# A two-layer hybrid diffusion block on one core: the order of TensorE's work in the attention stage

## The chip, the cores and the metric

The kernel runs on one core of a Trainium2 chip. The metric is the device time of one execution in microseconds; the time before is the median of three runs. The engines are named as in the profile: PE (TensorE matmul), DVE (VectorE), ACT (ScalarE), POOL (GpSimd), and SP, whose queue issues the DMAs.

## The reference

Two layers over 1024 latent and 256 context tokens of width 1024. Each layer: a modulated RMSNorm, one input projection whose columns are split among three groups, and one output projection with a gated residual.

```python
(xq, xk, xv, xz_a, xb, xa, xq_a, xkv_a, xz_b, xh, xbg, xcg, xz_c) = split_in(hx @ w_in)
...
o_ax, _, _ = gdn_bidir(*gdn_prepare(xq, xk, xv, xb, xa, ...), s_f, s_b)
a_x = gdn_output(o_ax, xz_a, gdn_norm_g)
...
k_x, v_x = mla_keys_values(xkv_a, mla_kv_norm_g, mla_w_kvb, cos, sin)
q_x = mla_queries(xq_a, mla_q_norm_g, mla_w_qb, cos, sin)
b_x = softmax_attention(q_x, concat([k_x, k_c]), concat([v_x, v_c])) * jax.nn.silu(xz_b)
c_x = conv_branch(xh, xbg, xcg, xz_c, conv_w)
x = x + gate_x * (concat([a_x, b_x, c_x]) @ w_out)
```

Group A is a gated delta recurrence (4 heads of 128, run forward and backward over chunks, the state handed from chunk to chunk). Group B is latent attention: 4 heads, 64 + 32 key columns, 64 value columns; latent queries read 1280 keys, and in the first layer the 256 context queries read the 256 context keys. Group C is a gated convolution. The second layer leaves the context rows out after the keys.

## The kernel before, in words

One Python program writes the instructions through the Tile framework, whose scheduler then orders each engine's instructions by its own estimate of when each is ready. The order in which the program writes them comes from the class `Sched` (L86): the main course of the program calls `sch.tick(us)` with its estimate of PE time, and every side lane (a Python generator: the recurrence, query rows, output weights, attention's ends) that is due runs on to its next `yield us`.

The attention stage goes by units: a query group of `GROUPS` (latent queries 0 to 511, 512 to 1023, context queries) times a pair of heads. Layer 0 has six units, layer 1 four. Per unit:

- `q_head` makes the query operand `qt` (hi and lo parts, 96 rows). Row 96 holds the shift: minus the largest score of the query.
- `a_max` (L1065 on) is the maxima pass: for each tile of 128 queries and each head, one matmul per key group (L1072) and a DVE reduction each (L1074), then a reduction over the groups (L1075) into `nm`. The maxima of the next unit are made during this one, two or three tiles after a step.
- `a_shift`: per head, four (context: two) PE transposes of one 128x1 column (L1082), and one ACT copy of 1x512 into row 96 of `qt` (L79 by its helper). It stands after the unit's last step.
- `a_scores` goes over the keys in steps of two key tiles: for two tiles and two heads, three matmuls (L84 by the helper `mm3`) and an exponential on ACT (L1096) into `probT`. A unit has five steps; a context unit has one.
- `a_pv`, called for a step after the scores of the next one: four V products (L1109), in which the two heads of a pair write to different column halves (`tile_position`), and the row sums: `probT` is added into `vt[5]` for head 0 on DVE (L1122) and into `vt[6]` for head 1 on POOL (L1120), 74 instructions each.
- `a_out` ends a unit as a lane: two ones products sum `vt` over its partitions (L1132), DVE takes the reciprocal (L1135) and multiplies (L1136), POOL multiplies by the gate (L1137), SP stores (L1138).

Beside this run two lanes of the recurrence (`recur`, one for each direction), with their PE groups at L1184, L1194, L1204, L1209 and L1210 and DVE work at L1186, L1196 and L1213. Each chunk has three handovers, with a `yield` after each:

```python
                    for h in range(4):
                        T.matmul(p3[:, h], lhsT=kq("k", h, i), rhs=Sd[:, h], start=True, stop=True)
                    for h in range(4):
                        V.scalar_tensor_tensor(out=X[:, h], in0=p3[:, h], scalar=negeg[:, i, g0 + h:g0 + h + 1], in1=X[:, h],
                                               op0=ALU.mult, op1=ALU.add)
...
                    yield 2.8
```

In the last units of a stage the recurrence has ended, and `load_wo` and `ahead` split the output projection's weights into hi and lo parts (ACT L75, POOL L76 as `wo_lo`) and start the projection.

Of the kernel before, what the change touches and what calls it, by code (L numbers as in the profile page):

```python
# [7 lines left out]
F32 = mybir.dt.float32  # L8
# [20 lines left out]
def kernel(  # L29
# [286 lines left out]
    for l in range(DEPTH):  # L316
# [539 lines left out]
        def q_head(g, h):  # L856
# [19 lines left out]
            Q[g, h] = dict(qt=qt, nm=st([128, 4], "st", name="nm"))  # L876
# [188 lines left out]
        def a_max(g, h, j):  # L1065
            q = Q[g, h]
            mx = st([128, 4], "st", name="mx")
            for gk, (t0, n) in enumerate(GROUPS):
                if g == 2 and gk < 2:
                    continue  # L1070
                pb = bank()
                T.matmul(pb[:, 0:n], lhsT=q["qt"][0:96, 0, j * 128:(j + 1) * 128],  # L1072
                         rhs=kh[0:96, h, t0:t0 + n] if gk < 2 else kc[0:96, 0, h, :], start=True, stop=True)
                V.tensor_reduce(mx[:, gk:gk + 1], pb[:, 0:n], AX.X, ALU.max)  # L1074
            V.tensor_reduce(q["nm"][:, j:j + 1], mx[:, 2 if g == 2 else 0:3], AX.X, ALU.max, negate=True)  # L1075

        def a_shift(g, h):
            q = Q[g, h]
# [6 lines left out]
        def a_scores(u, kts):  # L1085
# [12 lines left out]
            return pts  # L1098

        def a_pv(u, kts, pts):  # L1100
# [22 lines left out]

        def a_out(u):
# [4 lines left out]
            yield 1.5  # L1129
# [8 lines left out]
            S.dma_start(out=bx_d[pair, :, t0:t0 + n], in_=zb)  # L1138

# [12 lines left out]
        def recur(d):  # L1152
# [17 lines left out]
            for s, i in enumerate(order[d]):  # L1170
# [10 lines left out]
                if s:  # L1181
# [9 lines left out]
                    yield 2.8  # L1191
# [9 lines left out]
                yield 2.6  # L1201
# [28 lines left out]


        sch.add(recur(0), recur(1))
        units = [dict(g=g, pair=p) for g in qgs for p in range(2)]

# [3 lines left out]
        def maxes(u):  # L1238
            for j in range(GROUPS[u["g"]][1] // 128):
                for g, h in heads(u):  # L1240
                    yield a_max(g, h, j)

        def warm(u, vs):
# [3 lines left out]
            mg = maxes(u)  # L1247
            for i in vs:
                next(mg, None)
                v_tile(i)  # L1250
                sch.tick(0.9)
            for _ in mg:
                sch.tick(0.6)
# [14 lines left out]
        for u in units[:1 if last else 2]:  # L1268
            for gh in heads(u):
                a_shift(*gh)  # L1270
# [99 lines left out]
        prev = None  # L1370
        for x_, u in enumerate(units):
            g = u["g"]
            keys = a_keys(g)
            steps = [keys[q:q + 2] for q in range(0, len(keys), 2)]
            warmed = 1 if last else 2
            nxt = units[x_ + 1] if warmed <= x_ + 1 < nu else None
            mg = maxes(nxt) if nxt else None
            for q, kts in enumerate(steps):
                pts = a_scores(u, kts)
# [8 lines left out]
                if nxt:  # L1388
                    if q == 0:
                        sch.until(lambda: nxt["g"] in QA)  # L1390
                        for gh in heads(nxt):
                            q_head(*gh)
                        sch.tick(2.4)
                        if nxt["pair"] == 1 and nxt["g"] == 0:
                            sch.add(q_rows(1))
                    many = 8 if len(steps) == 1 else (0, 2, 3, 3, 0)[q]
                    for _ in range(many):
                        next(mg)
                        sch.tick(0.6)
                    if q == len(steps) - 1:  # L1400
                        for gh in heads(nxt):
                            a_shift(*gh)
# [4 lines left out]
        sch.add(a_out(prev[0]))  # L1407
        Q.clear()
        ahead(2)
        sch.tick(1.8)  # L1410
# [91 lines left out]
```

## Time and profile before

| | before |
|---|---|
| median of 3 runs | 1791.59 us (1791.51 to 1793.09) |
| the profiled execution, its own time | 1793.27 us |
| span of the profiled execution | 1791.6 us |
| mean granted TensorE clock | 0.979 of full speed |
| PE busy | 1720.9 us, 96% of the span |
| DVE busy | 1159.8 us, 65% |
| ACT busy | 766.1 us, 43% |
| POOL busy | 609.5 us, 34% |

The span is what the profile shows between the first and the last instruction; the execution's own time has 1.7 us more around it. Busy shares are averages over all stages. The attention stage of layer 0 lies at about 553 to 850 us, that of layer 1 at about 1419 to 1691 us. In rows of the trace a matmul with fp32 operands can appear as two records, and "x2" counts records; a group's busy time counts an overlap once.

### The profile page before, as it was taken

Reading aid. Unit: us, or ns where it says so; the run is one execution under the profiler, and the core shown is the slowest. Engines: PE = TensorE matmul, PEld = TensorE weight load, DVE = VectorE, ACT = ScalarE, POOL = GpSimd, SP = SyncE. Lnnn points to the kernel's source line nnn. Section 1 sums busy time; section 2 is a strip of 40 time slices with the busy share of each in tenths; the row PEclk is TensorE's granted clock in tenths of the full one; section 3 lists DMA queues with packets and bytes.
Section 4 is the critical chain, followed back from the end, with each engine's and each line's share of the span. In section 5 each row is a group of like instructions: output and inputs, shape, how many; then the busy total and the mean of one; then the engine's idle time right before and its main releaser. Section 6 shows DMA issues by size and latency. Waiting matters only on the chain.

```text
span 1791.6 us, 30054 instructions
## 1 busy us (share of the span) xinstructions
PE 1720.9 (96%) x11058; PEld 1336.6 (75%) x11058; DVE 1159.8 (65%) x2144; ACT 766.1 (43%) x1895; POOL 609.5 (34%) x811
## 2 busy tenths in 40 slices
PE   7999999999998799999999999998999889999998
PEld 5887887778888577664788987777787676776586
DVE  2445668887635766875666346689885487768565
ACT  4634663223436243254355435651244543424432
POOL 1510435222212232566431212463113323526741
PEclk9999999999999899999999999999999889999999
DMA  9333556552336446522543313556434524455541
GB/s 353 122 113 99 176 168 191 194 189 88 110 126 215 157 129 186 169 95 88 194 136 107 105 54 130 181 177 208 149 103 123 190 92 144 155 175 160 156 155 59
DMA packets 194578, 265.09 MB, mean 148 GB/s; under 512 B 50304, under 2 KB 114432, under 8 KB 194432
## 3 DMA queue, kind: packets, MB, share of 16 engines
q1 hardware_dynamic: 194432, 263.18, 45.3%
q8 instruction: 87, 1.43, 0.3%
q14 instruction: 59, 0.48, 0.1%
HBM read 183.76 MB, written 79.36 MB: 147 GB/s over the span
## 4 chain that ended last, share of the span: by engine, by line
PE 53%; DVE 5%; ACT 2%; issue 2%; DMA 2%; POOL 1%; SPq 0%; POOLq 0%; DVEq 0%; ACTq 0%
PE bank L84 20%; PE bank L448 13%; PE bank L1109 6%; PE bank L1072 2%; PE bank L1204 2%; PE bank L1194 2%; PE bank L1210 2%; PE bank L1209 2%; PE bank L1184 1%; DVE mx L1074 1%; DVE pr L676 1%; DVE Mb L677 1%; PE bank L512 1%; PE bank L1132 1%; DMA mb_d<-dg 1%
## 5 line engine op out<-in xcount | busy, mean ns | idle before, releaser
L448 PE MATMUL bank<-h_hi,w 128*128 128x512 f32 x1664 | 431.9, 402 | 2.5 <-DVE h_hi L283 2.5
L448 PEld LDWEIGHTS bank<-h_hi,w 128*128 128x128 f32 x1664 | 304.6, 189 | 74.8 <-issue 4.5
L448 PE MATMUL bank<-h_lo,w 128*128 128x512 f32 x832 | 217.7, 402 | 0.0
L448 PEld LDWEIGHTS bank<-h_lo,w 128*128 128x128 f32 x832 | 154.5, 190 | 37.2 <-issue 1.6
L462 DVE SCALAR_TENSOR_TENSOR acc<-pad,col,acc 128x1284 f32<-128x1284 f32 (+1 forms) x104 | 160.1, 1539 | 8.5 <-ACT acc L459 6.8
L1096 ACT ACTIVATE probT<-bank 128x512 f32<-128x512 f32 (+1 forms) x168 | 96.4, 590 | 129.0 <-PE bank L84 123.8
L84 PE MATMUL bank<-wo_hi,mix 128*128 128x512 f32 x576 | 142.8, 398 | 0.0
L84 PEld LDWEIGHTS bank<-wo_hi,mix 128*128 128x128 f32 x576 | 106.8, 188 | 25.5 <-issue 0.8
L1109 PE MATMUL bank<-probT,vt 128*64 128x512 f32 (+1 forms) x336 | 121.4, 601 | 1.1 <-ACT probT L1096 1.1
L76 DVE TENSOR_TENSOR w<-wr,w 128x1024 fp32r<-128x1024 f32 x52 | 66.4, 1279 | 85.2 <-ACT w L75 85.1
L1074 DVE TENSOR_REDUCE mx<-bank 128x1 f32<-128x512 f32 (+1 forms) x200 | 106.8, 588 | 12.8 <-PE bank L1072 11.9
L448 PE MATMUL bank<-h_c,w 128*128 128x256 f32 x816 | 109.5, 287 | 0.0
L1120 POOL TENSOR_TENSOR vt<-vt,probT 128x512 f32<-128x512 f32 x64 | 91.0, 1422 | 48.3 <-ACT probT L1096 45.7
L448 PEld LDWEIGHTS bank<-h_c,w 128*128 128x128 f32 x816 | 102.4, 190 | 6.2 <-issue 4.1
L1190 POOL TENSOR_TENSOR ring<-ring,qx 128x512 f32<-128x512 f32 x32 | 40.9, 1278 | 156.0 <-DMA ring<-row_d 121.9
L84 PE MATMUL bank<-qt,kh 97*128 97x512 f32 (+1 forms) x256 | 86.3, 419 | 3.3 <-ACT qt L79 3.2
L75 ACT ACTIVATE w<-wr 128x1024 fp32r<-128x1024 f32 x52 | 54.9, 1060 | 74.4 <-PE bank L448 55.4
L1122 DVE TENSOR_TENSOR vt<-vt,probT 128x512 f32<-128x512 f32 x64 | 68.3, 1068 | 18.7 <-ACT probT L1096 17.6
L1213 DVE SCALAR_TENSOR_TENSOR ring<-ring,gtot,bank 128x128 f32<-128x128 f32 x144 | 47.3, 345 | 42.6 <-PE bank L1209 33.6
L84 PE MATMUL bank<-wo_lo,mix 128*128 128x512 f32 x288 | 73.9, 395 | 0.0
L677 DVE TENSOR_TENSOR Mb<-Mb,pr 128x31 f32<-128x31 f32 (+15 forms) x186 | 68.8, 370 | 5.0
L676 DVE TENSOR_TENSOR pr<-L,Mb 128x31 f32<-128x31 f32 (+15 forms) x186 | 68.5, 368 | 4.5
(305 smaller groups left out, 3328.4 us busy)
## 6 DMA issues: line engine op xcount, KB each, us to landing
wr<-in_w_blk_dram SPq DMA_DIRECT2D x52, 512.0 KB, 4.0
wa<-in_w_ada_dram SPq DMA_DIRECT2D x32, 512.0 KB, 5.1
gcb<-row_d SPq DMA_DIRECT2D x20, 512.0 KB, 5.1
nn_d<-N SPq DMA_DIRECT2D x20, 512.0 KB, 3.3
ring<-vr_d SPq DMA_DIRECT2D x40, 256.0 KB, 2.6
ring<-nn_d SPq DMA_DIRECT2D x40, 256.0 KB, 3.4
ring<-kt_d SPq DMA_DIRECT2D x40, 256.0 KB, 5.1
qk_d<-gcb SPq DMA_DIRECT2D x18, 512.0 KB, 3.5
```

The source lines that it names most:

```text
L75: A.activation(out=hi, in_=raw, func=ACTF.Copy)
L76: eng.tensor_tensor(out=lo, in0=raw, in1=hi.bitcast(F32), op=ALU.subtract)
L84: T.matmul(outp, lhsT=lh, rhs=rh, start=q == 0, stop=q == n - 1)
L448: T.matmul(pb[:, 0:n], lhsT=self.w[:, wi, k, :], rhs=hg[g][hi][:, k, :], start=q + k == 0, stop=q == 2 and k == KD - 1)
L462: V.scalar_tensor_tensor(out=acc[:, 2:hi], in0=pad[:, 2 + t - r:hi + t - r], scalar=col[:, ci:ci + 1], in1=acc[:, 2:hi], op0=ALU.mult, op1 ...
L676: V.tensor_tensor(out=pv, in0=bc(L[:, 0:k, k], w), in1=N[:, k:k + 1, k:32].to_broadcast([128, k, w]), op=ALU.mult)
L677: V.tensor_tensor(out=N[:, 0:k, k:32], in0=N[:, 0:k, k:32], in1=pv, op=ALU.subtract)
L1074: V.tensor_reduce(mx[:, gk:gk + 1], pb[:, 0:n], AX.X, ALU.max)
L1096: A.activation(out=pts[r][:, kk, 0:n], in_=pb, func=ACTF.Exp)
L1109: T.matmul(u["po"][64 * r:64 * r + 64, 0:n], lhsT=vx[:, kt, hh * 64:hh * 64 + 64], rhs=pts[r][:, kk, 0:n], start=kt == keys[0], stop=kt == ...
L1120: P.tensor_tensor(acc, a0, a1, ALU.add)
L1122: V.tensor_tensor(out=acc, in0=a0, in1=a1, op=ALU.add)
```

## The change

In six parts:

1. PE's order is the order of the program from the moment when the recurrence lanes start until the attention stage has ended (`tc.manual_schedule` on PE). The other engines are ordered by the scheduler as before.
2. The maxima pass becomes a generator that stops after each key group's matmul. `filler` issues two of its matmuls after every score product of steps 1 to 3 (six in a context unit). The ticks are per score product.
3. `a_shift` is one transpose for both heads of a unit (a tile `nm` of 128 x 8), one ACT copy into `rw`, and two DMAs on SP's queue that write row 96 of `qt`. It stands ahead of the scores of the last step.
4. The row sums of both heads go to POOL (130 instructions), but those of head 0 in a unit's last step (18 on DVE).
5. `a_out` is no lane: its first part is called after the unit's last V products, its second (the sums matmul and what follows) ahead of the next V products.
6. The recurrence's yields are 3.4 and 3.0 in place of 2.8 and 2.6.

```diff
-        def a_shift(g, h):
-            q = Q[g, h]
-            n = GROUPS[g][1]
+        def a_shift(u):
+            m = GROUPS[u["g"]][1] // 128
             pn = bank()
-            for j in range(n // 128):
-                T.transpose(pn[0:1, j * 128:(j + 1) * 128], q["nm"][:, j:j + 1], ident)
-            copy_a(q["qt"][96:97, 0, 0:n], pn[0:1, 0:n])
+            T.transpose(pn[0:2 * m, 0:128], u["nm"][:, 0:2 * m], ident)
+            rw = st([8, 128], "h5", F32R, name="rw")
+            copy_a(rw[0:2 * m], pn[0:2 * m, 0:128])
+            for r, gh in enumerate(heads(u)):
+                S.dma_start(out=Q[gh]["qt"][96:97, 0, 0:128 * m].bitcast(F32).rearrange("p (j t) -> p j t", j=m), in_=rw[r * m:(r + 1) * m].bitcast(F32))
...
                     A.activation(out=pts[r][:, kk, 0:n], in_=pb, func=ACTF.Exp)
-                sch.tick(0.0028 * n)
+                    sch.tick(0.0014 * n)
+                    filler()
...
-                    if r:
+                    if kts[-1] == keys[-1] and r == 0:
+                        V.tensor_tensor(out=acc, in0=a0, in1=a1, op=ALU.add)
+                    else:
                         P.tensor_tensor(acc, a0, a1, ALU.add)
-                    else:
-                        V.tensor_tensor(out=acc, in0=a0, in1=a1, op=ALU.add)
...
-                    yield 2.8
+                    yield 3.4
...
-                yield 2.6
+                yield 3.0
...
         sch.add(recur(0), recur(1))
+        in_order = tc.manual_schedule(engines={mybir.EngineType.PE})
+        in_order.__enter__()
...
+            def filler():
+                if nxt and (len(steps) == 1 or 1 <= q <= 3):
+                    for _ in range(6 if len(steps) == 1 else 2):
+                        if next(mg, u) is not u:
+                            sch.tick(0.25)
...
+                if nxt and q == 4:
+                    a_shift(nxt)
+                pts = a_scores(u, kts, filler)
                 if prev:
+                    if ending:
+                        next(ending)
+                        ending = None
                     a_pv(*prev)
                     if prev[0] is not u:
-                        sch.add(a_out(prev[0]))
+                        ending = a_out(prev[0])
+                        next(ending)
...
+        in_order.__exit__(None, None, None)
```

Three pieces of the order show what that moves. In the rows a count stands at the end where an instruction repeats.

The first is PE in layer 0, at the end of the unit of latent queries 512 to 1023 and head pair 0: its last scores (L84), the shift (L1082, after L1088), the maxima (L1072, after L1077) and the V products (L1109, after L1119). Before:

```order
L84 MATMUL bank<-qt,kc 128x512 x12
L1082 MATMUL bank<-cst,nm 1x128 x3
L1109 MATMUL bank<-probT,vt 64x512
L1082 MATMUL bank<-cst,nm 1x128 x3
L1109 MATMUL bank<-probT,vt 64x512
L1082 MATMUL bank<-cst,nm 1x128
L1109 MATMUL bank<-probT,vt 64x512
L1082 MATMUL bank<-cst,nm 1x128
L1109 MATMUL bank<-probT,vt 64x512
```

and with the change:

```order
L84 MATMUL bank<-qt,kl 128x512
L1077 MATMUL bank<-kh,qt 128x512
L1077 MATMUL bank<-kc,qt 128x256
L1119 MATMUL bank<-probT,vt 64x512 x4
L1088 MATMUL bank<-cst,nm 8x128
L84 MATMUL bank<-qt,kc 128x512 x12
L1119 MATMUL bank<-probT,vt 64x512 x4
L84 MATMUL bank<-qt,kh 128x512 x2
L84 MATMUL bank<-qt,kl 128x512
```

The four V products of a step stand together, and one transpose ahead of the last scores takes the place of eight behind them. Over both stages the V products of before stand in 96 runs (64 single products, 15 of two, 5 of three, 9 of four, 1 of seven, 2 of eight); with the change in 40 (38 of four, 2 of eight).

The second is POOL in the last unit of layer 0: the row sums (L1120, after L1132), the gate (L1137, after L1147, first for the unit before, then for this one), and the output weights' splits (L76). Before:

```order
L1120 TENSOR_TENSOR vt<-probT 128x512
L1120 TENSOR_TENSOR vt<-vt,probT 128x512 x3
L1137 TENSOR_TENSOR zb<-zb,vt 128x512
L1120 TENSOR_TENSOR vt<-vt,probT 128x512 x4
L76 TENSOR_TENSOR mix<-raw,mix 128x512
L1120 TENSOR_TENSOR vt<-vt,probT 128x512
L76 TENSOR_TENSOR wo_lo<-wr,wo_hi 128x512 x5
L1137 TENSOR_TENSOR zb<-zb,vt 128x512
```

and with the change:

```order
L1132 TENSOR_TENSOR vt<-probT 128x512
L1132 TENSOR_TENSOR vt<-vt,probT 128x512 x2
L1132 TENSOR_TENSOR vt<-probT 128x512
L1132 TENSOR_TENSOR vt<-vt,probT 128x512 x2
L1147 TENSOR_TENSOR zb<-zb,vt 128x512
L1132 TENSOR_TENSOR vt<-vt,probT 128x512 x11
L76 TENSOR_TENSOR mix<-raw,mix 128x512
L76 TENSOR_TENSOR wo_lo<-wr,wo_hi 128x512 x3
L1147 TENSOR_TENSOR zb<-zb,vt 128x512
L76 TENSOR_TENSOR wo_lo<-wr,wo_hi 128x512 x3
```

Seventeen adds stand where nine stood, and five splits of weights move behind more of them.

The third is PE in layer 0 in the unit of latent queries 0 to 511 and head pair 0, where a recurrence group (L1184, after L1195) hands over through DVE to the next (L1194, after L1205). Before:

```order
L1184 MATMUL bank<-ring_5654,kx 128x128 x5
L1109 MATMUL bank<-probT,vt 64x512
L1184 MATMUL bank<-ring_5654,kx 128x128
L1109 MATMUL bank<-probT,vt 64x512
L1184 MATMUL bank<-ring_5654,kx 128x128 x2
L1072 MATMUL bank<-kh,qt 128x512
L1109 MATMUL bank<-probT,vt 64x512
L1072 MATMUL bank<-kh,qt 128x512
L1109 MATMUL bank<-probT,vt 64x512
L1072 MATMUL bank<-kc,qt 128x256
L1072 MATMUL bank<-kh,qt 128x512 x2
L1072 MATMUL bank<-kc,qt 128x256
```

and with the change:

```order
L1195 MATMUL bank<-ring_5654,kx 128x128 x8
L1077 MATMUL bank<-kh,qt 128x512
L84 MATMUL bank<-qt,kh 128x512 x2
L84 MATMUL bank<-qt,kl 128x512
L1077 MATMUL bank<-kc,qt 128x256
L1077 MATMUL bank<-kh,qt 128x512
L84 MATMUL bank<-qt,kh 128x512 x2
L84 MATMUL bank<-qt,kl 128x512
L1077 MATMUL bank<-kh,qt 128x512
L1077 MATMUL bank<-kc,qt 128x256
L1119 MATMUL bank<-probT,vt 64x512 x4
L1205 MATMUL bank<-ring_5653,ring_5654 128x128 x4
```

The recurrence group is no longer mixed with V products, and what stands between it and the next is fixed.

## Rows read from the trace of the kernel before

**Rows 1.** Page, busy time and share of each engine over the span.
```profile
PE 1720.9 (96%) x11058; PEld 1336.6 (75%) x11058; DVE 1159.8 (65%) x2144; ACT 766.1 (43%) x1895; POOL 609.5 (34%) x811
```

**Rows 2.** Windows: length, busy PE PEld DVE ACT POOL, clock, DMA share, GB/s.
```profile
553.00:632.00 79.00, 60.94 (x393) 51.03 (x392) 55.42 (x132) 29.80 (x79) 17.04 (x15) 0.87 0.58 198
...
781.00:824.00 43.00, 43.00 (x151) 21.53 (x149) 34.80 (x56) 25.69 (x64) 38.18 (x31) 1.00 0.39 123
824.00:850.00 26.00, 26.00 (x88) 10.38 (x88) 14.55 (x15) 9.03 (x16) 14.14 (x11) 1.00 0.22 71
1419.00:1466.00 47.00, 34.20 (x172) 27.70 (x173) 38.12 (x78) 24.61 (x57) 15.42 (x12) 0.79 0.49 158
```

**Rows 3.** Both stages' V products by form; windows of the last units.
```profile
L1109 PE MATMUL bank<-probT,vt 128*64 128x512 f32 x160 | 60.9, 612 | 1.1 <-ACT probT L1096 1.1
...
L1109 PE MATMUL bank<-probT,vt 128*64 128x512 f32 x160 | 57.7, 611 | 0.0
...
781.00:824.00 43.00, 17.59 (x40) 3.53 (x40) 1.00 0.39 123
824.00:850.00 26.00, 14.33 (x40) 3.10 (x40) 1.00 0.22 71
```

**Rows 4.** Timeline of PE in a step with scattered V products: start, us, instruction.
```profile
804.08 1.07 PE L1109 MATMUL bank<-probT,vt 128*64 128x512 f32 x2
805.08 0.49 PE L1072 MATMUL bank<-kh,qt 96*128 96x512 f32 x1
...
806.62 0.73 PE L1072 MATMUL bank<-kh,qt 96*128 96x512 f32 x2
807.29 1.07 PE L1109 MATMUL bank<-probT,vt 128*64 128x512 f32 x2
...
810.29 2.96 PE L84 MATMUL bank<-qt,kc 97*128 97x512 f32 x12
813.09 0.49 PE L1082 MATMUL bank<-cst,nm 128*1 128x128 f32 x3
```

**Rows 5.** Timeline of PE where four V products stand in a row.
```profile
1480.15 1.94 PE L1109 MATMUL bank<-probT,vt 128*64 128x512 f32 x8
1482.02 0.33 PE L846 MATMUL bank<-cst,mq 128*128 128x128 f32 x1
```

**Rows 6.** Groups by form, the shift's transposes in layers 0 and 1.
```profile
L1082 PE MATMUL bank<-cst,nm 128*1 128x128 f32 x40 | 7.4, 298 | 3.7 <-DVE nm L1075 3.7
...
L1082 PE MATMUL bank<-cst,nm 128*1 128x128 f32 x32 | 4.6, 272 | 0.0
```

**Rows 7.** The shift's ACT copies by form, and PE's timeline in layer 1's opening.
```profile
L79 ACT ACTIVATE qt<-bank 1x512 fp32r<-1x512 f32 x6 | 3.5, 584 | 4.3 <-PE bank L1082 4.2
...
1464.13 1.12 PE L84 MATMUL bank<-qt,kh 97*128 97x512 f32 x2 [2.05 <-ACT qt L79]
```

**Rows 8.** DVE and POOL groups by form, 640 to 850; POOL's adds.
```profile
L1122 DVE TENSOR_TENSOR vt<-vt,probT 128x512 f32<-128x512 f32 x32 | 34.4, 1076 | 9.0 <-ACT probT L1096 8.5
L1074 DVE TENSOR_REDUCE mx<-bank 128x1 f32<-128x512 f32 x48 | 31.3, 682 | 3.1 <-PE bank L1072 2.8
L1213 DVE SCALAR_TENSOR_TENSOR ring<-ring,gtot,bank 128x128 f32<-128x128 f32 x56 | 18.5, 346 | 18.2 <-PE bank L1209 15.4
...
L1074 DVE TENSOR_REDUCE mx<-bank 128x1 f32<-128x256 f32 x24 | 10.0, 416 | 1.8 <-PE bank L1072 1.8
...
L1120 POOL TENSOR_TENSOR vt<-vt,probT 128x512 f32<-128x512 f32 x31 | 43.7, 1409 | 18.5 <-ACT probT L1096 17.1
L76 POOL TENSOR_TENSOR wo_lo<-wr,wo_hi 128x512 fp32r<-128x512 f32 x11 | 15.6, 1427 | 5.7 <-ACT wo_hi L75 5.5
...
L1120 POOL TENSOR_TENSOR vt<-vt,probT x64: 1261/1283/1778, 655.4 to 1685.3; 128x512 f32<-128x512 f32 x64
```

**Rows 9.** DMA issues (KB, us to landing); SP's waits, 760 to 870.
```profile
bx_d<-zb SPq DMA_DIRECT2D x8, 256.0 KB, 2.0
...
SPq L1138 <- POOL zb L1137: 22.2, 2, 21.3
```

More of the change, by code (lines that the diff above doesn't have):

```diff
@@ L1077, in a_shift, with a_max @@
-        def a_shift(g, h):
-            q = Q[g, h]
-            n = GROUPS[g][1]
-            pn = bank()
-            for j in range(n // 128):
-                T.transpose(pn[0:1, j * 128:(j + 1) * 128], q["nm"][:, j:j + 1], ident)
-            copy_a(q["qt"][96:97, 0, 0:n], pn[0:1, 0:n])
-        def a_scores(u, kts):
+        def a_max(u):
+            g = u["g"]
+            m = GROUPS[g][1] // 128
+            nm = u["nm"] = st([128, 8], "st", name="nm")
+            for j in range(m):
+                for r in range(2):
+                    h = 2 * u["pair"] + r
+                    mx = st([128, 4], "st", name="mx")
+                    for gk, (t0, n) in enumerate(GROUPS):
+                        if g == 2 and gk < 2:
+                            continue
+                        pb = bank()
+                        T.matmul(pb[:, 0:n], lhsT=Q[g, h]["qt"][0:96, 0, j * 128:(j + 1) * 128],
+                                 rhs=kh[0:96, h, t0:t0 + n] if gk < 2 else kc[0:96, 0, h, :], start=True, stop=True)
+                        V.tensor_reduce(mx[:, gk:gk + 1], pb[:, 0:n], AX.X, ALU.max)
+                        if gk < 2:
+                            yield
+                    V.tensor_reduce(nm[:, r * m + j:r * m + j + 1], mx[:, 2 if g == 2 else 0:3], AX.X, ALU.max, negate=True)
+                    yield
@@ L1236, in heads @@
             return [(u["g"], 2 * u["pair"] + r) for r in range(2)]
[L1238 to L1241, printed above, removed]
         def warm(u, vs):
@@ L1246, in warm @@
             sch.tick(2.4)
-            mg = maxes(u)
+            mg = a_max(u)
             for i in vs:
-                next(mg, None)
+                for _ in range(2):
+                    next(mg, None)
                 v_tile(i)
-                sch.tick(0.9)
+                sch.tick(0.8)
             for _ in mg:
-                sch.tick(0.6)
+                sch.tick(0.25)
+            a_shift(u)
         k_pair(0)
@@ L1267 @@
             sch.add(q_rows(0))
-        for u in units[:1 if last else 2]:
-            for gh in heads(u):
-                a_shift(*gh)
         nu = len(units)
@@ L1369 @@
         sch.add(load_wo())
-        prev = None
+        prev = ending = None
         for x_, u in enumerate(units):
-            g = u["g"]
-            keys = a_keys(g)
+            keys = a_keys(u["g"])
             steps = [keys[q:q + 2] for q in range(0, len(keys), 2)]
-            warmed = 1 if last else 2
-            nxt = units[x_ + 1] if warmed <= x_ + 1 < nu else None
-            mg = maxes(nxt) if nxt else None
-            for q, kts in enumerate(steps):
-                pts = a_scores(u, kts)
+            nxt = units[x_ + 1] if (1 if last else 2) <= x_ + 1 < nu else None
+            if nxt:
+                mg = a_max(nxt)
+            def filler():
+                if nxt and (len(steps) == 1 or 1 <= q <= 3):
+                    for _ in range(6 if len(steps) == 1 else 2):
+                        if next(mg, u) is not u:
+                            sch.tick(0.25)
+            for q, kts in enumerate(steps):
+                if nxt and q == 0:
+                    sch.until(lambda: nxt["g"] in QA)
+                    for gh in heads(nxt):
+                        q_head(*gh)
+                    sch.tick(2.4)
+                    if nxt["pair"] == 1 and nxt["g"] == 0:
+                        sch.add(q_rows(1))
+                if nxt and q == 4:
+                    a_shift(nxt)
+                pts = a_scores(u, kts, filler)
                 if prev:
+                    if ending:
+                        next(ending)
+                        ending = None
                     a_pv(*prev)
                     if prev[0] is not u:
-                        sch.add(a_out(prev[0]))
+                        ending = a_out(prev[0])
+                        next(ending)
                         for gh in heads(prev[0]):
@@ L1387 @@
                 prev = (u, kts, pts)
[L1388 to L1402, printed above, removed]
+                if nxt and len(steps) == 1:
+                    for _ in mg:
+                        pass
+                    a_shift(nxt)
                 if x_ == nu - 1 and q in (1, 3):
@@ L1406 @@
         a_pv(*prev)
-        sch.add(a_out(prev[0]))
+        ending = a_out(prev[0])
+        next(ending)
         Q.clear()
         ahead(2)
+        sch.tick(2.0)
+        next(ending)
+        in_order.__exit__(None, None, None)
         sch.tick(1.8)
```

16 lines of the change are left out of this document (4 added, 12 removed).

## The prediction

> **What bounds the kernel now.** I read the page first: TensorE (PE) is busy for 96% of the span [rows 1]; no other engine is above 65%. So only time taken out of PE's own stream, or gaps put into it, can move the end. Then the windows of the two attention stages [rows 2], one row per piece of a stage. PE has idle time only where a stage opens: 79.00 - 60.94 = 18.1 us of the first 79 us in layer 0, and 47.00 - 34.20 = 12.8 us of the first 47 us in layer 1. In the last two units of layer 0 (781 to 850) PE is busy throughout, VectorE (DVE) has slack, and GpSimd (POOL) is busy 38.18 + 14.14 = 52.3 of 69 us. The granted clock there is 1.00, the upper level of 2.4 GHz; in the openings it is 0.87 and 0.79. So the question has two halves: how much PE time do badly placed instructions cost, and who makes PE wait once its order is fixed?
>
> **V products.** The trace shows a product as two records. 320 records in the two stages take 60.9 + 57.7 = 118.6 us [rows 3], that is 160 products of 0.741 us. The reason for the high mean is in the timeline: a single product between other matmuls holds PE from 804.08 to 805.08, 1.00 us [rows 4], while four products in a row run from 1480.15 to 1482.02, 1.87 us, 0.468 us each [rows 5]. In a row, the products of the two heads, which lie in different column halves, run side by side; a single one has no partner. In the order of before 64 of 96 runs are singles; in the order of the change 38 of 40 runs are of four and two of eight, as the first piece of the order shows. So 160 x 0.468 = 74.9 us, **-43.7 us**.
>
> **Fewer runs.** Other matmuls beside a V run pay too. Two maxima matmuls between two singles take 807.29 - 806.62 = 0.67 us, while score matmuls in a run take (813.09 - 810.29) / 12 = 0.233 us each [rows 4], 0.47 us for two. So a run costs its neighbours about 0.2 us, and 96 - 40 = 56 runs go: **-11 us** (between 0 and -11, since the two may share an edge).
>
> **Shift rows.** 72 transposes took 7.4 + 4.6 = 12.0 us [rows 6]. Ten remain, of up to eight columns each. A wider transpose is in no row; between the 0.27 us of a narrow one and the 0.741 us of a mean V product I take 0.45 us, near the narrow one since the free size, 128, is the same: 4.5 us. **-7 us** (-9 to -4). The ScalarE copies of 1x512 (0.584 us, [rows 7]) become one shorter copy per unit, beside PE; ScalarE has slack, so nothing.
>
> Gross, then: -62 us. What comes back:
>
> **Row sums on POOL.** 56 adds leave DVE (74 to 18) and 56 join POOL (74 to 130). DVE was not the bound, so its 56 x 1.076 = 60 us are worth nothing directly [rows 8]; they make room for reductions. POOL's price is 1.409 us. In the last two units of layer 0 POOL then needs 52.3 + 14 x 1.409 = 72 us, while PE's own work there shrinks from 69 to about 53 us: the 40 products of these two units (80 records) take 17.59 + 14.33 = 31.9 us now [rows 3] and 40 x 0.468 = 18.7 us in a row, and fewer runs and transposes give some 3 us. POOL is therefore late at the end. Part of this is taken up before: POOL can run on beside the output projection, whose weight splits it also makes (1.427 us each). Bounds are 0 (all taken up) and 72 - 53 = 19 us per layer. The work in POOL's queue that PE truly needs is from the sums matmul of the last but one unit to that of the last: 16 adds, 4 weight splits and some 5 us of small work, 16 x 1.409 + 4 x 1.427 + 5 = 33 us, against 28 us of PE. That gives some 6 us. Layer 1 has weight splits behind the adds too, with the same result. **+12 us** (0 to 38).
>
> **Shift by DMA.** Twenty small DMAs are added on SP's queue. The path is transpose, ScalarE copy, DMA, scores: 0.45 + 0.58 + 2.0 us, the last from the nearest DMA in the trace, a store of 256 KB that lands in 2.0 us [rows 9]. Ahead of the first scores that need it stand the last step's twelve score matmuls and four V products, 12 x 0.233 + 1.87 = 4.7 us, so 3.0 us is covered, with 1.7 us to spare. The cover fails where SP is blocked: before, SP once stood 21.3 us behind a store that waited for POOL [rows 9]. In the new program that store lies some twenty us ahead of the next shift. Also the transpose itself now waits, in order, for the last reduction (0.416 to 0.682 us and a queue of up to two), of which the V products ahead of it (1.87 us) cover most. Behind a shift's DMA SP issues the recurrence's loads, which a late ScalarE copy would delay; they are issued a chunk ahead of their use, so I put nothing on that. Eight units at 1 us: **+8 us** (0 to 30, the upper end being one block as in the row, plus the transposes).
>
> **The recurrence in program order.** The change fixes PE's order while two recurrence lanes hand over between PE and DVE. Two directions x ten chunks x three handovers in two layers, in pairs, make 60. After a handover PE must find 8 DVE instructions done, 8 x 0.346 = 2.77 us [rows 8]; before, the scheduler put other work there. The new waits in the lanes, 3.4 and 3.0 us instead of 2.8 and 2.6, put at least a step's scores in between, 12 x 0.233 = 2.80 us; in the third piece of the order it is nine full maxima and score matmuls, two short ones (0.12 us, by half the columns) and four V products, some 4.2 us. So a narrow place can miss by a reduction (0.682 us) queued on DVE. One in six missing by 0.6 us: **+6 us** (0 to 60, at 1 us each).
>
> **Openings.** The stages open with PE waiting for shift rows: 2.05 us on the ScalarE copy in layer 1 [rows 7]. Now one unit's shift goes out inside the warm-up, earlier, but through a DMA, and the in-order stream cannot step past it. **+1 us** (-4 to +6).
>
> **Maxima spread singly.** Two maxima (0.233 us each) follow a score product. PE spends 20 matmuls of 0.233 and 1.87 us, 6.5 us, on such a step; DVE needs eight reductions of 0.682 or 0.416 us, about 5.0 us with the small ones. Nothing, while DVE has no adds there; that cover is what the moved adds buy.
>
> The sum: -43.7 - 11 - 7 + 12 + 8 + 6 + 1 = -34.7 us. Against the profiled execution's 1793.3 us this is 1758.6 us; the median of the runs is 1.7 us lower. **Forecast 1758 us.** A measurement here tells 0.2%, about 3.6 us, from no change.
>
> **Rivals.**
> *POOL becomes the bound.* For: the slowest add in the trace took 1.778 us [rows 8], and the adds now follow each other. Then the 64 adds of the four units without a recurrence cost 64 x 0.37 = 24 us more, all in view: 1782 us. Against: most adds took 1.283 us. It shows as PE waiting for POOL's adds at the sums matmul.
> *POOL at twice DVE's price.* At 2 x 1.076 = 2.15 us, 64 adds cost 64 x 0.74 = 47 us more: 1805 us. Against: POOL's measured mean is 1.409 / 1.076 = 1.3 times that of DVE. The Trainium skill, GPSIMD Engine Reference, section "Engine selection", says that adds of two tiles belong on VectorE and run about half as fast on GpSimd; by that rule this change would be slower, and the trace's ratio of 1.3 speaks against taking it at its full price.
> *PE waits at the handovers (slower).* One mechanism: a fixed order holds up everything behind a recurrence product whose operand DVE has not finished. Without this term the sum is -40.7 us, so it decides from 40.7 / 60 = 0.68 us per handover. At 1.0 us each it gives +19 us, 1811 us. For: the margin is 2.80 against 2.77 us at the narrowest. Against: the DVE has lost 60 us of adds, and most places are as wide as 4.2 us.
> *Little is given back.* POOL catches up, shifts are covered: -62 us + 4 us, 1735 us. For: PE was not idle at all in the last two units [rows 2], though its stream there was as tight.
> *No change.* Grouping saves nothing net because each term that comes back lies at its upper third: about 1792 us. That the order does not change is excluded by the pieces of the order shown.
>
> **Chances.** Forecast's case 0.54 (1742 to 1774 us), POOL as bound 0.12, POOL at twice the price 0.02, handovers 0.13, little given back 0.14, no change 0.05. Faster by over 0.2%: 0.54 + 0.12 + 0.14 = 0.80; same 0.05; slower 0.15. The range reaches from half of the low case to just past the POOL case: 1736 to 1786 us. Left out are half of the low case, the two slow ones: about 0.2.
>
> **What would show it.** V records in runs of eight, each run 1.9 us; their sum near 75 us; maxima in pairs at 0.47 us. If POOL limits, PE's idle time sits at the sums matmuls and the projection's second half, released by POOL. If handovers limit, it sits ahead of the recurrence products, released by DVE. If the shifts limit, it sits ahead of the first score matmul of a unit, released by a DMA, or at the transposes. The forecast is wrong if the V records do not shrink by 35 us or more, or if PE's idle time in the attention stages grows by more than 50 us.

## The result, and the profile after

The changed kernel takes 1746.83 us in the median of four runs (1746.53 to 1753.43); the kernel before took 1792.34 us beside it (1791.51 to 1794.29). The ratio is 0.9753 (95% interval 0.9729 to 0.9778): 45 us faster, where 34 were forecast, inside the range of 1736 to 1786 us. The profiled execution took 1746.92 us with a span of 1745.2 us.

Of its page, the busy time and share of each engine, which answers to [rows 1]:

```profile
PE 1661.4 (95%) x10996; PEld 1321.9 (76%) x10996; DVE 1119.6 (64%) x2088; ACT 756.2 (43%) x1885; POOL 664.2 (38%) x867
```

PE's busy time fell by 1720.9 - 1661.4 = 59.5 us. Outside its busy time PE spent 1791.6 - 1720.9 = 70.7 us before and spends 1745.2 - 1661.4 = 83.8 us now, 13.1 us more. 59.5 - 13.1 is the whole 46.4 us of span. So the change takes busy time out of PE and gives a little back as waits.

Where the busy time went shows in the groups by form of the two attention stages: V products first (as [rows 3], layer 0, then layer 1), then the shift's transposes (as [rows 6]).

```profile
L1119 PE MATMUL bank<-probT,vt 128*64 128x512 f32 x160 | 41.5, 624 | 0.0
...
L1119 PE MATMUL bank<-probT,vt 128*64 128x512 f32 x160 | 39.1, 603 | 0.0
...
L1088 PE MATMUL bank<-cst,nm 128*8 128x128 f32 x4 | 1.1, 273 | 0.5 <-DVE nm L1082 0.5
L1088 PE MATMUL bank<-cst,nm 128*4 128x128 f32 x2 | 0.6, 320 | 3.8 <-DVE nm L1082 3.8
...
L1088 PE MATMUL bank<-cst,nm 128*8 128x128 f32 x4 | 1.2, 298 | 3.8 <-DVE nm L1082 3.8
```

The 160 V products take 80.6 us in place of 118.6 us, though a record lasts as long as ever (624 and 603 ns; 612 and 611 before): they lie over each other now. A group of four holds PE for 1.87 us, as the timeline of one in mid-stage shows (start, us, instruction):

```profile
723.09 1.94 PE L1119 MATMUL bank<-probT,vt 128*64 128x512 f32 x8
724.96 2.05 PE L1205 MATMUL bank<-ring 128*128 128x128 f32 x16
```

Where the waits came from shows in PE's waits: first over the attention stage of layer 0, then of layer 1 (waiting line, releaser: us in total, times, longest).

```profile
PE bank L1142 <- ACT probT L1105: 4.4, 1, 4.4
PE bank L1088 <- DVE nm L1082: 4.3, 2, 3.8
PE bank L1077 <- ACT qt L79: 3.3, 3, 1.7
PE bank L1142 <- POOL vt L1132: 3.2, 1, 3.2
...
PE bank L84 <- DMA qt<-rw: 0.6, 1, 0.6
...
PE bank L1077 <- ACT qt L79: 7.7, 1, 7.7
PE bank L1142 <- DVE vt L1130: 7.3, 1, 7.3
PE bank L1088 <- DVE nm L1082: 3.8, 1, 3.8
...
PE bank L1077 <- DVE ring L1197: 1.1, 2, 0.6
PE bank L1195 <- DVE ring L1224: 0.3, 1, 0.3
```

Three of these rows are new and large: the sums matmuls (L1142) near the end of each stage wait 4.4 + 3.2 us and 7.3 us, 14.9 us together. (The 7.7 us in the opening of layer 1 were 6.0 us before.) In layer 0 these are the sums of the last but one unit, and those of the last wait for nothing; in layer 1 they are those of the last. The releasers differ, but POOL has a part in all three. The timelines show in layer 0 ACT, whose exponentials wait for a buffer that POOL still reads, and POOL's adds, the first of which ends at about the start of the second sums matmul (797.44); then in layer 1 POOL, seven adds in one piece, and DVE, whose first add of the last step waits for one of them.

```profile
791.67 2.07 ACT L1105 ACTIVATE probT<-bank 128x512 f32<-128x512 f32 x4 [1.39 <-POOL vt L1132]
...
796.13 2.48 POOL L1132 TENSOR_TENSOR vt<-vt,probT 128x512 f32<-128x512 f32 x2
...
1627.07 9.08 POOL L1132 TENSOR_TENSOR vt<-vt,probT 128x512 f32<-128x512 f32 x7
...
1634.96 1.73 DVE L1130 TENSOR_TENSOR vt<-vt,probT 128x512 f32<-128x512 f32 x1 [1.40 <-POOL vt L1132]
1636.62 1.75 DVE L76 TENSOR_TENSOR mix<-raw,mix 128x512 fp32r<-128x512 f32 x1
1638.29 1.75 DVE L1130 TENSOR_TENSOR vt<-vt,probT 128x512 f32<-128x512 f32 x1
...
1644.60 0.69 DVE L76 TENSOR_TENSOR mix<-raw,mix 128x512 fp32r<-128x512 f32 x1 [0.70 <-ACT mix L75]
```

Of the 7.3 us in layer 1 (1632.78 to 1640.09) only the first 2.2 us pass before DVE can start. The rest is three instructions on DVE, two adds and a split between them, at 1.73 to 1.75 us each while POOL works; the same split took 0.69 us at 1644.60, when POOL stood idle.

A wait costs more than its length. These windows (length, busy time of PE, PEld, DVE, ACT and POOL, granted clock, DMA share, GB/s) lie before and behind the waits at the end of layer 0:

```profile
780.00:788.00 8.00, 7.96 (x34) 4.86 (x32) 2.81 (x6) 5.49 (x21) 7.72 (x10) 1.00 0.35 99
792.30:795.50 3.20, 1.94 (x2) 0.29 (x2) 1.92 (x2) 1.44 (x3) 3.15 (x3) 0.50 0.00 0
797.40:800.60 3.20, 3.16 (x8) 1.00 (x9) 1.15 (x1) 0.00 (x0) 2.32 (x2) 0.50 0.00 0
```

Ahead of the wait of 4.4 us the granted clock is 1.00, the upper level of 2.4 GHz; behind it 0.50, the level of 1.2 GHz. The sums matmul and the V group after the second wait hold PE from 797.44 to 802.50, 5.1 us, where elsewhere a sums matmul takes 1.00 us (819.38 to 820.38) and a group 1.87 us.

### The profile page after: what moved, and what is told of

The parts are those of the page before. It is cut to its first block, busy times and chain, and to the rows that moved or that the text cites. A ratio compares the mean times of both kernels' runs of the same rounds, so it can differ in the third digit from the quotient of the medians.

```text
span 1745.2 us, 29978 instructions
## 1 busy us (share of the span) xinstructions
PE 1661.4 (95%) x10996; PEld 1321.9 (76%) x10996; DVE 1119.6 (64%) x2088; ACT 756.2 (43%) x1885; POOL 664.2 (38%) x867
## 4 chain that ended last, share of the span: by engine, by line
PE 55%; DVE 6%; issue 3%; ACT 3%; DMA 3%; POOL 2%; SPq 0%; POOLq 0%; DVEq 0%; ACTq 0%
PE bank L84 20%; PE bank L448 15%; PE bank L1119 4%; PE bank L1205 2%; PE bank L1215 2%; PE bank L1221 2%; PE bank L1220 2%; PE bank L1195 2%; PE bank L1077 2%; DVE mx L1079 1%; DVE pr L676 1%; POOL vt L1132 1%; DVE Mb L677 1%; PE bank L1142 1%; PE bank L512 1%
## 5 line engine op out<-in xcount | busy, mean ns | idle before, releaser
L1132 POOL TENSOR_TENSOR vt<-vt,probT 128x512 f32<-128x512 f32 x112 | 144.4, 1309 | 14.0 <-ACT probT L1105 13.3
L84 PE MATMUL bank<-wo_hi,mix 128*128 128x512 f32 x576 | 144.1, 400 | 0.0
L84 PEld LDWEIGHTS bank<-wo_hi,mix 128*128 128x128 f32 x576 | 107.7, 190 | 26.6 <-ACT mix L75 0.8
L76 DVE TENSOR_TENSOR w<-wr,w 128x1024 fp32r<-128x1024 f32 x52 | 66.7, 1284 | 85.2 <-ACT w L75 85.2
L84 PE MATMUL bank<-qt,kh 97*128 97x512 f32 (+1 forms) x256 | 83.5, 407 | 1.1 <-DMA qt<-rw 0.6
L1119 PE MATMUL bank<-probT,vt 128*64 128x512 f32 (+1 forms) x336 | 82.7, 602 | 0.0
L84 PE MATMUL bank<-wo_lo,mix 128*128 128x512 f32 x288 | 73.9, 395 | 0.0
L613 POOL TENSOR_TENSOR gcb<-gcb,gc 128x1024 f32<-128x1024 f32 x20 | 44.8, 2242 | 61.8 <-DMA gcb<-row_d 47.7
```

Of the source, the lines that this page charges most:

```text
L76: eng.tensor_tensor(out=lo, in0=raw, in1=hi.bitcast(F32), op=ALU.subtract)
L84: T.matmul(outp, lhsT=lh, rhs=rh, start=q == 0, stop=q == n - 1)
L1119: T.matmul(u["po"][64 * r:64 * r + 64, 0:n], lhsT=vx[:, kt, hh * 64:hh * 64 + 64], rhs=pts[r][:, kk, 0:n], start=kt == keys[0], stop=kt == ...
```

## The experiments

Twelve variants were timed, each in four runs, four variants and the kernel before on one chip at a time. Ratios are to the kernel before on the same chip.

| variant | median us | ratio (95% interval) |
|---|---|---|
| the change | 1746.83 | 0.9753 (0.9729 to 0.9778) |
| 1 head by head | 1749.74 | 0.9763 (0.9744 to 0.9782) |
| 2 scheduler's order | 1777.88 | 0.9928 (0.9907 to 0.9948) |
| 3 last unit on DVE | 1741.51 | 0.9716 (0.9697 to 0.9736) |
| 4 first shift later | 1745.42 | 0.9744 (0.9722 to 0.9765) |
| 5 before, in program order | 1778.55 | 0.9923 (0.9893 to 0.9953) |
| 6 adds split throughout | 1748.40 | 0.9749 (0.9729 to 0.9769) |
| 7 column transposes | 1751.78 | 0.9772 (0.9744 to 0.9799) |
| 8 short yields | 1756.67 | 0.9798 (0.9775 to 0.9820) |
| 9 two banks | 1752.42 | 0.9775 (0.9760 to 0.9790) |
| 10 two banks, same half | 1801.64 | 1.0052 (1.0034 to 1.0069) |
| 11 last two units on DVE | 1742.74 | 0.9717 (0.9698 to 0.9737) |
| 12 as 11, both shifts later | 1737.84 | 0.9688 (0.9665 to 0.9712) |

### Is it the order? (2 and 5)

Variant 2 takes the fixed order away and leaves all else:

```diff
-        in_order = tc.manual_schedule(engines={mybir.EngineType.PE})
-        in_order.__enter__()
...
-        in_order.__exit__(None, None, None)
```

> The changed kernel without the fixed order on TensorE: the scheduler orders it as before, all else (maxima spread, shift by DMA, adds on POOL, yields) stays. V products then stand in 85 runs, 55 of them single. Theory (the order is what pays): V products back to about 0.70 us each and the edges back, +30 to +40 us, 1777 to 1787 us. Rival (the other parts pay, and the order costs or gives nothing): 1740 to 1752 us.

Measured: 1777.88 us, in the theory's range. V products by form, layer 0, then layer 1:

```profile
L1119 PE MATMUL bank<-probT,vt 128*64 128x512 f32 x160 | 61.0, 630 | 0.5 <-ACT probT L1105 0.5
...
L1119 PE MATMUL bank<-probT,vt 128*64 128x512 f32 x160 | 56.8, 608 | 0.0
```

117.8 us, about what they cost before (118.6 us). Without the order the rest of the change is worth 0.7%.

Variant 5 adds the order alone to the kernel before:

```diff
         sch.add(recur(0), recur(1))
+        in_order = tc.manual_schedule(engines={mybir.EngineType.PE})
+        in_order.__enter__()
...
+        sch.tick(2.0)
+        in_order.__exit__(None, None, None)
```

> The kernel before with one part of the change alone: TensorE in program order over the same stretch. That program already writes the four V products of a step together, so they stand in 40 runs; the maxima stay in blocks of two or three tiles, the transposes of single columns and the adds on VectorE stay. Theory (the order alone gives the V products' 35 us and most of the edges' 10 us, and the rest of the change keeps PE fed): 35 to 45 us gained, 10 to 20 given back to waits at the maxima and transposes, 1757 to 1772 us. Rival (without the spread maxima the fixed order stalls on reductions and hands all of it back): 1785 us or more.

Measured: 1778.55 us, between theory and rival. Its V products by form (layer 0; layer 1 reads the same), the page's busy times, and the two largest of PE's waits in layer 0:

```profile
L1109 PE MATMUL bank<-probT,vt 128*64 128x512 f32 x160 | 38.5, 604 | 0.0
...
PE 1686.9 (95%) x11058; PEld 1336.6 (75%) x11058; DVE 1164.3 (65%) x2144; ACT 767.1 (43%) x1895; POOL 607.7 (34%) x811
...
PE bank L1072 <- DVE mx L1074: 9.2, 3, 7.0
PE bank L1082 <- DVE nm L1075: 5.4, 3, 2.6
```

The order alone gives all of the V products' saving (77.0 us), but the span of this execution is 1785.0 us, so PE spends 98.1 us outside its busy time against 70.7 us before, 27 us more. (This execution was the slowest of the four, 8 us above the median.) In layer 0 the largest of these waits are for reductions of maxima made in blocks, 9.2 + 5.4 us. So the order and the rest of the change need each other: either alone is worth some 0.75%, both 2.5%. Which part of the rest the order needs is argued only by elimination: with the adds, the transposes or the yields put back one at a time (variants 6, 7 and 8 below) the change loses 0 to 8 us, and by the ratios 30 us lie between it and variant 5. That leaves the spread maxima, the shift's place and the new course of `a_out`; no run takes the spreading alone away.

### What does a group of four buy? (1, 9 and 10)

Variant 1 keeps the groups and changes the order in them:

```diff
-            for kk, kt in enumerate(kts):
-                for r in range(2):
+            for r in range(2):
+                for kk, kt in enumerate(kts):
```

> The changed kernel with one edit: in each group of four V products the two of head 0 come first, then the two of head 1. The runs stay runs of four, so the number of their edges is the same; only one neighbouring pair in a group lies in different column halves instead of three. Theory (products in different column halves run side by side, and that is what grouping buys): only the middle pair of a group overlaps, a group takes about 1.0 + 0.94 + 1.0 = 2.9 us instead of 1.9 us, 40 full groups: +40 us, 1787 us. Rival (what grouping buys is only that there are fewer edges between kinds of matmul): 1747 us, within 3 us.

Measured: 1749.74 us, the rival's time. By form, layer 0: 41.9 us for the same 160 records. Taken alone, that speaks against products running side by side. But it only shows that neighbours in program order need not be partners. Variants 9 and 10 take the halves themselves away. Both give each head a PSUM bank; 10 also puts both heads into columns 0 to 63:

```diff
-                u["po"] = bank()
+                u["po"] = [bank(), bank()]
...
-                    T.matmul(u["po"][64 * r:64 * r + 64, 0:n], ..., tile_position=(0, 64 * r))
+                    T.matmul(u["po"][r][0:64, 0:n], ..., tile_position=(0, 0))
```

> The changed kernel with the V products of the two heads accumulated in a PSUM bank each, still in different column halves; the last multiply of a unit on VectorE becomes two. This is the control for the next run: it changes the banks and not the halves. Expected by all theories: a group of four V products takes 1.9 us as before, one more bank is held, 1747 to 1753 us.

> The same kernel as in the run beside it, two banks, but both heads' V products go through the same column half (columns 0 to 63). Runs of four stay runs of four, their edges stay. Theory (a pass of a V product takes 0.43 us by itself, and two heads' products start together only because they use different halves; grouping buys the partner): a group of four takes 8 x 0.43 + 0.1 = 3.5 us instead of 1.9 us, 40 full groups, +65 us against the run beside it, 1810 to 1820 us. Rival (grouping buys only fewer edges): as the run beside it, within 4 us.

Measured: 1752.42 us for the control, 1801.64 us for the same half. The same group of four in both timelines, with what follows it, the control first:

```profile
816.12 1.94 PE L1119 MATMUL bank<-probT,vt 128*64 128x512 f32 x8
817.99 3.07 PE L84 MATMUL bank<-qt,kc 97*128 97x512 f32 x12
```

```profile
832.16 3.65 PE L1119 MATMUL bank<-probT,vt 128*64 128x512 f32 x8
835.74 3.08 PE L84 MATMUL bank<-qt,kc 97*128 97x512 f32 x12
```

1.87 us against 3.58 us, with the same edges. By form the V products take 43.0 + 38.4 = 81.4 us in the control and 73.1 + 72.6 = 145.7 us in variant 10: 64.3 us, the 65 us of the expectation. So the partner in the other half is what a group buys, and variant 1 shows that it may stand two places further on in the stream. The Trainium skill, TensorEngine Tiling (Array Packing), section "Key Properties", states that tiles operate independently, so that different ones can load weights and multiply in parallel; variants 1 and 10 agree. The total rose by 49 us only, since PE's time outside busy fell from 1751.5 - 1666.5 = 85.0 to 1797.1 - 1728.5 = 68.6 us: a slower PE waits less for POOL. The sums matmuls wait 3.4 + 1.2 + 6.6 us in the control and not at all in variant 10.

### Row sums: POOL or DVE? (6, 3 and 11)

Each changes one condition; 6, 3 and 11 in this order:

```diff
-                    if kts[-1] == keys[-1] and r == 0:
+                    if r == 0:
...
+                    if r == 0 and (kts[-1] == keys[-1] or u is units[-1]):
...
+                    if r == 0 and (kts[-1] == keys[-1] or any(u is w for w in units[-2:])):
```

> The changed kernel with the row sums of head 0 on VectorE throughout, as before. Theory (VectorE needs about 5.0 us for a step's reductions, and two more adds of 1.08 us make it 7.2 against PE's 6.5, so PE waits in steps with maxima, up to 0.7 x 24 steps = 17 us, while POOL's 15 us at the ends are saved): 1733 to 1752 us, with PE idle before maxima, released by reductions. Rival (VectorE has room and the move to POOL only costs): 1731 to 1735 us, with no idle time before maxima.

> The changed kernel, but in the last unit of each layer head 0's row sums go to VectorE again, as in the kernel before; there are no maxima in that unit. Theory (PE's idle 4.4 + 3.2 us in layer 0 and 7.3 us in layer 1 at the sums matmuls is POOL running late behind its adds): most of 15 us goes, 1732 to 1738 us. Rival (the projection's weight splits or the unit's finishing chain are late anyway): 1743 to 1747 us.

> The changed kernel, but head 0's row sums go to VectorE in the last two units of each layer. Theory (POOL's lateness at the end builds up over the last two units: in layer 0 PE also waits 4.4 us for an exponential whose buffer POOL still reads): 10 to 14 us less than the changed kernel, 1733 to 1737 us, idle time at the sums matmuls under 3 us a layer. Rival (VectorE, with reductions in the last but one unit, becomes late instead and PE waits before maxima, as in the run with all adds split): 1740 to 1748 us.

Measured: 1748.40, 1741.51 and 1742.74 us. The move to POOL is worth nothing in sum: variant 6 without it has the same ratio as the change. Its time lies in the theory's range, but PE waits only 0.9 us before maxima for reductions, not up to 17 us. Its waits are others. At the sums matmuls only 2.5 us are left, in layer 1, but others stand in mid-stage and at the weights' splits (PE's timeline):

```profile
648.47 1.72 PE L1205 MATMUL bank<-ring 128*128 128x128 f32 x13 [1.39 <-DVE ring L1197]
...
1636.77 1.07 PE L1142 MATMUL bank<-vt,cst 128*64 128x512 f32 x2 [2.47 <-DVE vt L1130]
...
1645.16 3.81 PE L84 MATMUL bank<-wo_hi,mix 128*128 128x512 f32 x9 [2.34 <-ACT wo_hi L75]
```

Variant 3 is 0.37% better than the change by the ratios (about 6.6 us; the intervals just overlap), half of what the theory expected. In layer 1 it cuts 7.3 us to 2.6 us. In layer 0 the 4.4 us stay, since they arise in the unit before the last. Variant 11 removes those, and gains nothing more. Its two largest new waits, and what ACT does ahead of them, are

```profile
770.62 0.63 ACT L75 ACTIVATE wo_hi<-wr 128x512 fp32r<-128x512 f32 x1 [2.04 <-DMA wr<-in_w_out_dram]
772.31 0.63 ACT L75 ACTIVATE wo_hi<-wr 128x512 fp32r<-128x512 f32 x1 [1.06 <-DMA wr<-in_w_out_dram]
772.85 0.58 ACT L1105 ACTIVATE probT<-bank 128x512 f32<-128x512 f32 x1
773.48 1.22 PE L84 MATMUL bank<-qt,kh 97*128 97x512 f32 x2 [2.64 <-ACT probT L1105]
...
1640.30 2.59 ACT L75 ACTIVATE wo_hi<-wr 128x512 fp32r<-128x512 f32 x4 [3.77 <-DMA wr<-in_w_out_dram]
1640.98 2.37 PE L84 MATMUL bank<-wo_hi,mix 128*128 128x512 f32 x9 [3.06 <-ACT wo_hi L75]
```

So the rival's time held, but not its reason: PE waits only 1.9 us for reductions of maxima. Next behind the adds come ACT's splits of the weights, which wait for the weights' DMA and hold up an exponential that stands behind them.

### Openings, shift and yields (4, 12, 7 and 8)

Variants 4 and 12 move the shift of the openings behind other matmuls (12 on top of 11):

```diff
-            a_shift(u)
...
         k_pair(2)
         sch.tick(1.7)
+        a_shift(units[0])
...
+                if x_ == 0 and not last:
+                    a_shift(units[1])
```

In variant 4 the second unit's shift stays in place; the last two lines are 12's.

> The changed kernel, but the first unit's shift stands behind the second half of the key products instead of right behind its own maxima. Theory (the fixed order makes PE wait 3.8 us in each layer for the last negated maxima, and the moved matmuls cover it): 5 to 8 us less, 1739 to 1742 us. Rival (the wait only moves to the scores, which then wait for the DMA, or PE's clock rises later): 1745 to 1749 us.

> The run before with the openings changed as well: in layer 1 the first shift stands behind the second half of the key products, and in layer 0 the second unit's shift, which is the one that waits 3.8 us for its negated maxima, stands behind the first unit's scores. Theory (the moved matmuls cover the wait): 3 to 6 us less than the run beside it, 1728 to 1733 us. Rival (the openings are bound by the chain of reductions and copies, and the wait moves to the next matmul): within 2 us of the run beside it.

Measured: 1745.42 us for 4, in the rival's range. In layer 0 the shift that waits is the second unit's, which 4 does not move, and in layer 1 half of the wait is left:

```profile
582.88 0.27 PE L1088 MATMUL bank<-cst,nm 128*4 128x128 f32 x1 [3.67 <-DVE nm L1082]
...
1433.85 0.27 PE L1088 MATMUL bank<-cst,nm 128*8 128x128 f32 x1 [1.89 <-DVE nm L1082]
```

Variant 12 moves both and takes 1737.84 us, 5 us less than variant 11 beside it, the difference that the theory had; the time itself lies above its range. The times still overlap (1731.8 to 1740.5 us against 1738.9 to 1744.4 us). The transposes wait 1.1 + 0.3 us now, against 4.7 + 3.8 us in variant 11. Against the change its interval lies wholly below: it is the best version here, 12 us better by the ratios.

Variant 7 makes the shift of single columns again, in the change's place:

```diff
-            T.transpose(pn[0:2 * m, 0:128], u["nm"][:, 0:2 * m], ident)
...
+                for j in range(m):
+                    T.transpose(pn[0:1, j * 128:(j + 1) * 128], u["nm"][:, r * m + j:r * m + j + 1], ident)
+                copy_a(Q[gh]["qt"][96:97, 0, 0:128 * m], pn[0:1, 0:128 * m])
```

> The changed kernel with the shift made as before, by a transpose of one column for each query tile and head and a ScalarE copy into the operand, without the DMA; its place in the program stays. Theory (62 more transposes at 0.13 to 0.17 us on PE, no DMA wait saved, since that was 0.6 us): +7 to +11 us, 1754 to 1758 us. Rival (the DMA's latency is what costs, and saving it pays for the transposes): 1742 to 1748 us.

Measured: 1751.78 us, between theory and rival, by the ratios 3.4 us more than the change, with overlapping intervals. The transposes take 5.8 + 4.8 = 10.6 us by form against 2.9 us; the total shows about half of that.

Variant 8 puts the recurrence's yields back to 2.8 and 2.6.

```diff
-                    yield 3.4
+                    yield 2.8
...
-                yield 3.0
+                yield 2.6
```

> The changed kernel with the recurrence's waits at their old values, 2.8 and 2.6 instead of 3.4 and 3.0. Theory (handovers had almost no idle time at the new values, 1.9 us in all, and the old ones still leave a step's scores in between): 1745 to 1753 us. Rival (the margin of a handover is what the new values buy, and without it PE waits in program order at most of them): 60 handovers at 0.4 us or more, 1770 us or more, with PE idle before the recurrence's products, released by VectorE.

Measured: 1756.67 us, above the theory's range, 8 us more than the change by the ratios (the intervals just touch), and far from the rival's 1770 us. PE's waits in layer 0 name where:

```profile
PE bank L1142 <- DVE vt L1130: 5.4, 2, 5.1
PE bank L1077 <- ACT qt L79: 4.6, 3, 2.6
...
PE bank L1077 <- DVE ring L1197: 0.4, 1, 0.4
```

No handover in layer 0 waits over 0.4 us. How shorter yields cost 8 us is open: they move everything in the program, and the profiled execution, 1752.5 us, was the shortest of its four.

## Why the prediction was right, point by point

The sum of the prediction beside the profiled execution, in us:

| term | forecast | measured |
|---|---|---|
| V products | -43.7 | 80.6 - 118.6 = -38.0 |
| fewer runs | -11 | the remainder of PE's busy time, -12.4 |
| shift rows | -7 | 2.9 - 12.0 = -9.1 |
| gross | -62 | -59.5 |
| POOL late at the ends | +12 | +14.9 |
| shift by DMA, openings, handovers | +15 | the remainder of PE's time outside busy, -1.8 |
| net | -34.7 | -46.4 (spans) |

The two remainders are differences and not measurements of the terms beside them. The 12 us by which the change beat the forecast come from the second: it is 17 us better than the +15, while the gross gain and POOL are 5 us worse.

- **V products.** The mechanism held, and variant 10 shows it. The size was 6 us off: the forecast priced every product at 0.468 us, from one group's distance to the next instruction. Measured by form, it is 80.6 / 160 = 0.504 us, records that last beyond that point included. Variant 5, with as many runs, takes 38.5 us a layer; most of what the change has above that, 41.5 us in layer 0, is the one group that ran at the low clock.
- **Fewer runs.** The price of a run is borne out, the total is not shown. In PE's timeline after the change a score product's last matmul takes 0.33 us ahead of a group and 0.23 us elsewhere, its first two 0.57 us behind a group and 0.46 us elsewhere, 0.2 us a run:

```profile
805.16 0.40 PE L84 MATMUL bank<-qt,kl 96*128 96x512 f32 x1
805.49 1.94 PE L1119 MATMUL bank<-probT,vt 128*64 128x512 f32 x8
807.35 0.73 PE L84 MATMUL bank<-qt,kh 97*128 97x512 f32 x2
807.92 0.39 PE L84 MATMUL bank<-qt,kl 96*128 96x512 f32 x1
808.15 0.63 PE L84 MATMUL bank<-qt,kh 97*128 97x512 f32 x2
808.61 0.40 PE L84 MATMUL bank<-qt,kl 96*128 96x512 f32 x1
```

But the remainder of -12.4 us follows other things too. Variant 2, with 85 runs, has -10.6 us (1700.4 - 1720.9 us of busy time, less 0.8 us of V products and 9.1 us of transposes), and variant 5, with 40, has +8.5 us. That it lies so near to -11 is in part luck.
- **Shift rows.** Right within 2 us. A wide transpose takes 0.27 to 0.32 us, like a narrow one, and not 0.45 us.
- **POOL.** The size was right, 14.9 us of waits at the sums matmuls. The place was right in layer 1, where 7.3 us stand between the last two units' sums, for the 6 us that were priced there. In layer 0 it was luck: that stretch shows no wait, and the 7.6 us stand at the sums of the last but one unit. The 28 us of PE in this working rest on no row. The term also left out that the granted clock drops to 0.50 behind the waits. The adds took 1.309 us on POOL, not the slowest add's 1.778 us, so that rival fell, though its sign, waits at the sums matmuls, came. The Trainium skill, GPSIMD Engine Reference, section "Engine selection", has such adds at about half of VectorE's speed; the groups by form give 1.309 us on POOL after the change and 1.080 us on DVE in variant 6, 1.2 times; only DVE's fastest add, 0.62 us in variant 12 against POOL's fastest of 1.26 us, bears the page out. In variant 6 DVE's adds and splits of this size took 0.62 to 0.69 us where no such instruction ran on POOL, and up to 1.82 us beside one. The 1805 us of that price did not come.
- **Shift by DMA (+8) and handovers (+6)** are the steps that failed, both in size. In steady state no transpose waits over 0.6 us, and the DMA is waited for once, 0.6 us: the cover of 4.7 us stood. The waits for the recurrence's DVE work come to 1.1 + 0.3 us in layer 1 and none in layer 0. The handover's margin, 2.80 against 2.77 us, was taken at the narrowest place and with both lanes due together. It was also priced too small: 8 x 0.346 us adds up the durations of records that overlap, and eight of these instructions in a row took 2.16 us in the trace of before:

```profile
644.55 2.16 DVE L1213 SCALAR_TENSOR_TENSOR ring<-ring,gtot,bank 128x128 f32<-128x128 f32 x8
```

The slower rival fell with it, as variant 8 shows even with shorter yields. PE's waits for the recurrence's loads, 4.0 us in layer 0 before, are gone as well; they are in the remainder of -1.8 us.
- **Openings (+1).** PE waits 3.8 us in each layer for negated maxima; before, it waited 3.7 us for them in layer 0, and in layer 1 2.05 us for the copied shift [rows 7]. Variant 12 shows that these waits can be covered.
- **Maxima for nothing.** Right: PE waits 0.2 us for reductions of single maxima in layer 0 after the change. That spreading also saves time is argued only, from the 9.2 us that variant 5, with maxima in blocks, waits there. But the text gave the credit to the moved adds; variant 6 shows that the steps keep up nearly as well without them.

## What to carry to other kernels

Matmuls of half the columns are cheap only beside a partner for the other half: group them, and look at the time from the group's start to the next instruction, not at the duration of a record. A fixed order pays when the rest of the program is written for it, so that each wait finds cover in the stream; the order alone and the rest alone each gave under a third of the whole here. Work moved to an idle engine is free until the stage's end, where its queue comes due: look at the last two units, and at what the waits there do to the clock. When you price a row of short instructions, take the length of the row and not the sum of its records.

## What the runs showed of the hardware that was not expected

- Products of two heads overlapped as well when all of one head's stood ahead of the other's: 41.9 us for 160 records against 41.5 us when they alternated.
- Raising the V products' price by 64.3 us (by form) lengthened the kernel by 49 us only, since 16 us of PE's time outside busy went.
- Behind a wait of 4.4 us the granted clock was 0.50, and it was still 0.50 behind a second wait of 3.2 us: a sums matmul and a V group took 5.1 us, against 2.9 us elsewhere.
- DVE's instructions of two 128x512 inputs took 0.69 us with POOL idle and up to 1.75 us with POOL at work on adds or splits of that size, so work moved to POOL can also slow DVE.
